# Routed experts: only the filled slots of a tile are gathered and stored, by indirect transfers with a bound

## The chip, the cores and the metric

The kernel is one program on one core of a Trainium2 chip. The core has five engines with a queue each: PE (matrix multiply into PSUM), DVE (VectorE), ACT (ScalarE), POOL (GpSimd) and SP (which issues DMAs here). DMAs issued from any of them run on the core's 16 DMA engines. The metric is the device time of one execution in microseconds, as a median of several runs.

## The reference

A long network for 512 tokens of width 1024: a first block (four mixers and a feed-forward part), then two transformer layers over 512 tokens plus, in layer 0, 256 context tokens. Each of the two layers ends in a mixture of experts, and that is all the change touches. Each token goes to two of 16 experts (1024 to 256 to 1024), and all tokens to one shared expert:

```python
idx = grp[:, None] * EXPERTS_PER_GROUP + local          # two experts for each token
wts = wts / jnp.sum(wts, axis=-1, keepdims=True)
combine = jnp.einsum('tk,tke->te', wts, jax.nn.one_hot(idx, N_EXPERTS, dtype=jnp.float32))
y = jnp.einsum('tef,efd->td', jax.nn.silu(g) * u * combine[..., None], prm['w_down'])
y = y + (jax.nn.silu(t @ prm['sh_gate']) * (t @ prm['sh_up'])) @ prm['sh_down']
```

## The kernel before

`moe` runs once for each layer (768 tokens in layer 0, 512 in layer 1). `route` (from L1899) sorts the pairs of token and expert into tiles of 128 slots: tile s < 16 belongs to expert s, its filled slots first; pairs beyond the 128th of an expert go to overflow tiles, of which layer 0 always runs one (tile 16) and a loop `For_i` (L2184) any further ones. It makes two tables: `idx` (L1997), for each slot of each tile the token whose row it takes, with token 0 in empty slots, and `sli` (L1975), for each token and each of its two experts the slot that holds its result.

`expert` (L2018 to L2069) is a generator in three parts for one tile. First POOL gathers 128 rows of `h2` (4 KB each, in DRAM) into `xe` by an indirect DMA (L2025), PE transposes them in eight pieces (L2039) and ACT and DVE split each into a high and a low part. Then the gate and up weights are loaded by `wpart` (SP, L2082, two halves of 512 KB into one buffer of 1 MB), split likewise (ACT L208, DVE L209), and multiplied in three products for each pair of parts (`mm3`, L186 to L188). Then the down weights, and the result `ye` of 128x1024, which ACT copies out of PSUM (L2067) and SP stores to `yslot`, a DRAM tensor with one row for each slot (L2068). The loop in `moe` (L2168 to L2180) interleaves the parts of neighbouring tiles, and in six tiles of layer 0 and four of layer 1 a piece of the shared expert's product (`shared_down`). The weights have several buffers, so SP issues loads as early as a buffer is free; SP's queue runs in the order in which it was written, and so does POOL's.

Behind the loop, `gather(t)` (L2196) fetches for each token tile the two rows of each token from `yslot` by two indirect DMAs on POOL (L2199), and ACT and DVE weigh and add them (L2207 to L2210). In layer 0 `l1_open` goes on to the next norm (scale rows `nsc`, loaded by POOL); in layer 1 the sum is stored as the output and the kernel ends. Empty overflow slots are read by nobody's result, but `zeros` fills their rows of `yslot` at the start (L1850). Instructions are put in order by a scheduler that honours data dependences and priorities.

## Time and profile before

| | us |
|---|---|
| median of 3 runs | 2537.07 |
| lowest and highest of them | 2532.33, 2540.72 |
| the profiled execution | 2529.52 |
| its span, first to last instruction | 2527.8 |

Engine times are sums of busy time over the span; a PE instruction's busy time runs to the modelled end of its pipeline, so neighbours overlap. Idle time is shown with what ended it. The times of the sections below are from the profiled execution, in microseconds from the start of the span.

### The profile page before, as it was taken

The page shows a single profiled execution, that of the slowest core. Times are in us where ns is not written, and L with a number is a line of the kernel's source. Part 1 is how long each engine was busy: PE and PEld are TensorE (multiplying, and loading weights), DVE is VectorE, ACT ScalarE, POOL GpSimd, SP SyncE. Part 2 cuts the span into 40 slices and gives each one's busy share as a digit, 9 for nine tenths or more (in the row PEclk, how much of TensorE's full clock was granted, in tenths as well). Part 3 has the DMA queues.
Part 4 walks back from the last instruction along what each step waited for, and adds up shares of the span by engine and source line. Part 5 has one row for each costly group of instructions (what it writes and reads, how often), then busy time and mean ns, then how long its engine had stood idle before and what let it go on. Part 6 is the DMA issues. An engine that isn't in the chain of part 4 may idle for free. (4 is left out here: it accounts for less than half of the span.)

```text
span 2527.8 us, 37507 instructions
## 1 busy us (share of the span) xinstructions
PE 2277.4 (90%) x14345; PEld 1808.3 (72%) x14345; DVE 1545.7 (61%) x2915; ACT 1109.3 (44%) x1836; POOL 321.7 (13%) x409
## 2 busy tenths in 40 slices
PE   8959999999988999988999998898994989998994
PEld 6836577888876677766788886697773767687773
DVE  4455654323324455645676648967876987666885
ACT  4435533212223233433445433336774456624773
POOL 0001201000000000011111114200113113301112
PEclk9979989999999999955999999989997999998997
DMA  5345535233325656453545426639996220056995
GB/s 166 100 166 173 190 136 196 88 109 100 101 61 189 224 191 218 125 125 73 113 112 124 102 59 183 236 130 341 342 340 225 97 67 1 1 171 206 375 365 191
DMA packets 367793, 411.55 MB, mean 163 GB/s; under 512 B 117476, under 2 KB 299172, under 8 KB 361468
## 3 DMA queue, kind: packets, MB, share of 16 engines
q1 hardware_dynamic: 356972, 370.83, 46.4%
q0 software_dynamic: 10640, 38.31, 4.1%
q8 instruction: 114, 1.87, 0.3%
q14 instruction: 67, 0.55, 0.1%
HBM read 340.46 MB, written 70.65 MB: 163 GB/s over the span
## 5 line engine op out<-in xcount | busy, mean ns | idle before, releaser
L304 DVE TENSOR_REDUCE mx<-s 128x1 f32<-128x768 f32 (+4 forms) x160 | 121.4, 760 | 85.9 <-PE s L188 65.3
L209 DVE TENSOR_TENSOR eg_l<-eg_w,eg_h 128x2048 fp32r<-128x2048 f32 x66 | 151.0, 2289 | 19.5 <-ACT eg_h L208 19.3
L208 ACT ACTIVATE eg_h<-eg_w 128x2048 fp32r<-128x2048 f32 x66 | 126.5, 1918 | 28.7 <-DMA eg_w<-in_moe_w_up_dram 12.2
L186 PE MATMUL p<-lhh,abw_hi 128*128 128x512 f32 (+1 forms) x336 | 115.3, 343 | 0.8 <-ACT l0n1tmp L241 0.8
L188 PE MATMUL p<-lhh,abw_lo 128*128 128x512 f32 (+1 forms) x336 | 114.5, 341 | 1.6 <-DVE abw_lo L209 1.6
L187 PE MATMUL p<-lhl,abw_hi 128*128 128x512 f32 (+1 forms) x336 | 114.7, 341 | 0.0
L187 PE MATMUL g<-eg_l,xh 128*128 128x512 f32 x264 | 107.1, 406 | 5.5 <-DVE eg_l L209 5.0
L186 PE MATMUL g<-eg_h,xh 128*128 128x512 f32 x264 | 107.6, 408 | 3.8 <-ACT eg_h L208 3.8
L188 PE MATMUL g<-eg_h,xl 128*128 128x512 f32 x264 | 104.4, 395 | 0.0
L209 DVE TENSOR_TENSOR ed_l<-ed_w,ed_h 128x2048 fp32r<-128x2048 f32 x33 | 75.6, 2292 | 44.1 <-ACT ed_h L208 44.1
L882 PE MATMUL adaps<-adaw,silu_c 128*32 128x512 f32 x384 | 75.3, 640 | 29.6 <-DMA adaw<-in_ada_w_dram 29.6
L994 POOL COPY ms<-mc 128x2 f32<-128x2 f32 x30 | 9.1, 304 | 635.0 <-ACT mc L989 620.1
L2025 POOL DMA_INDIRECT xe<-h2d,idx x33 | 45.9, 1392 | 310.0 <-PE x L2039 243.4
L186 PEld LDWEIGHTS p<-lhh,abw_hi 128*128 128x128 f32 (+1 forms) x336 | 61.8, 184 | 23.9 <-issue 8.0
L310 POOL TENSOR_SCALAR ap<-ap,rc 128x768 f32<-128x768 f32 x64 | 58.4, 913 | 153.7 <-DVE rc L307 92.0
L310 POOL TENSOR_SCALAR mlp<-mlp,rc 128x768 f32<-128x768 f32 (+1 forms) x48 | 41.5, 864 | 250.8 <-DVE rc L307 200.4
L186 PE MATMUL p<-h2h,wg_hi 128*128 128x512 f32 x176 | 69.5, 395 | 0.6 <-ACT h2h L234 0.6
L188 PEld LDWEIGHTS p<-lhh,abw_lo 128*128 128x128 f32 (+1 forms) x336 | 62.3, 185 | 10.1 <-DVE abw_lo L209 2.0
L187 PE MATMUL p<-h2l,wg_hi 128*128 128x512 f32 x176 | 69.1, 393 | 0.0
L188 PE MATMUL p<-h2h,wg_lo 128*128 128x512 f32 x176 | 69.0, 392 | 0.0
L186 PE MATMUL p<-wd_hi,ah 128*128 128x512 f32 x176 | 68.5, 389 | 0.2 <-DVE x L836 0.2
L186 PE MATMUL p<-h2h,wu_hi 128*128 128x512 f32 x176 | 68.7, 390 | 0.0
(750 smaller groups left out, 6770.4 us busy)
## 6 DMA issues: line engine op xcount, KB each, us to landing
adaw<-in_ada_w_dram SPq DMA_DIRECT2D x48, 1024.0 KB
eg_w<-in_moe_w_gate_dram SPq DMA_DIRECT2D x66, 512.0 KB
eg_w<-in_moe_w_up_dram SPq DMA_DIRECT2D x66, 512.0 KB
ed_w<-in_moe_w_down_dram SPq DMA_DIRECT2D x33, 1024.0 KB
yslot<-ye SPq DMA_DIRECT2D x33, 512.0 KB
wg_w<-in_w_gate_up_dram SPq DMA_DIRECT2D x11, 1024.0 KB
wu_w<-in_w_gate_up_dram SPq DMA_DIRECT2D x11, 1024.0 KB
wd_w<-in_w_down_dram SPq DMA_DIRECT2D x10, 1024.0 KB
```

The lines of the kernel that those rows point to most:

```text
L186: mm(out, lh, rh, start=start, stop=False)
L187: mm(out, lh, rl, start=False, stop=False)
L188: mm(out, ll, rh, start=False, stop=stop)
L208: self.nc.scalar.activation(hi, raw, AF.Copy)
L209: self.nc.vector.tensor_sub(lo, raw, hi.bitcast(F32))
L304: nc.vector.tensor_reduce(mx, s, axis=AX.X, op=OP.max, negate=True)
L310: nc.gpsimd.tensor_scalar(pout, pout, rc, 1.0, op0=OP.mult, op1=OP.mult)
L882: nc.tensor.matmul(self.ada_ps[32 * j:32 * j + 32], self.silu_c[:, k], w[:, j * 512:(j + 1) * 512], start=k == 0, stop=k == 7, tile_positi ...
L994: nc.gpsimd.tensor_copy(s[:, a:b:b - a - 1], c[:, a + 1:b - 1:b - a - 3])
L2025: nc.gpsimd.indirect_dma_start(out=x, out_offset=None, in_=h2, in_offset=bass.IndirectOffsetOnAxis(ap=idx, axis=0))
```

## The change

The tables become one: `idx` holds for each slot the output row 2 x token + choice (`idx[:, 1]`) and half of it, the token (`idx[:, 0]`); an empty slot gets 8191, beyond the bound. The gather skips rows beyond the bound. The two buffers `xe` are made once for each layer and cleared, since skipped rows keep what they held. The result is written from POOL by an indirect DMA with a bound, straight to row 2 x token + choice of `yrow` (1536 rows). The combination then needs no indices: one DMA of 1 MB from SP for each token tile brings both rows of each token. The zero fill of `yslot` goes.

```diff
@@ -1845,9 +1845,7 @@
-        self.yslot = self.dram.tile([27 * P, D], F32, name="yslot")
-        for i in range(16, 27):
-            nc.gpsimd.dma_start(self.yslot[i * P:(i + 1) * P], z)
+        self.yrow = self.dram.tile([2 * 768, D], F32, name="yrow")
@@ -1855,8 +1853,8 @@
                                 compare_op=OP.is_gt, fill=0.0)
-        self.tokid = self.ct([P, 6], "tokid")
-        nc.gpsimd.iota(self.tokid, pattern=[[P, 6]], base=0, channel_multiplier=1,
+        self.rowid = self.ct([P, 2, 6], "rowid")
+        nc.gpsimd.iota(self.rowid, pattern=[[1, 2], [2 * P, 6]], base=1, channel_multiplier=2,
                        allow_small_or_imprecise_dtypes=True)
@@ -1971,8 +1969,9 @@
         nc.vector.tensor_reduce(sl, so, axis=AX.X, op=OP.add)
-        sli = pool.tile([P, 2, nt], I32, name="sli")
+        sli = wp.tile([P, 2, nt], I32, name="sli")
         nc.vector.tensor_copy(sli, sl)
@@ -1985,7 +1984,7 @@
                                 count[:, None, :27].to_broadcast([P, n, 27]), op=OP.is_equal)
-        nc.vector.tensor_mul(til, til, self.tokid[:, None, :nt, None].to_broadcast([P, 2, nt, 27]))
+        nc.vector.tensor_mul(til, til, self.rowid[:, :, :nt, None].to_broadcast([P, 2, nt, 27]))
         ip = self.pt("r")
@@ -1993,8 +1992,13 @@
             nc.tensor.matmul(ip[:, :27], row[:, i % 4], tf[:, i], start=i == 0, stop=i == n - 1)
-        idx = pool.tile([P, 27], I32, name=f"idx{l}")
-        nc.vector.tensor_copy(idx, ip[:, :27])
+        rows = wp.tile([P, 2, 27], F32, name="rrows")
+        nc.vector.tensor_copy(rows[:, 0], ip[:, :27])
+        nc.vector.tensor_scalar(rows[:, 1], rows[:, 0], 0.0, 8192.0, op0=OP.is_equal, op1=OP.mult)
+        nc.vector.scalar_tensor_tensor(rows[:, 0], rows[:, 0], -1.0, rows[:, 1], op0=OP.add, op1=OP.add)
+        idx = pool.tile([P, 2, 27], I32, name=f"idx{l}")
+        nc.vector.tensor_copy(idx[:, 1], rows[:, 0])
+        nc.vector.tensor_scalar(idx[:, 0], idx[:, 1], 1, None, op0=OP.arith_shift_right)
@@ -2013,17 +2017,17 @@
         nc.vector.tensor_copy(eidi, eid)
-        return wts, sli, eidi, idx
-
-    def expert(self, l, h2, idx, e, ydst, wp, wq):
+        return wts, eidi, idx
+    def expert(self, l, h2, tok, row, nt, e, wp, wq):
...
         raws, parts, xs = wq
-        p, n0 = xs[self.slots % len(xs)]
+        x = xs[self.slots % len(xs)]
         self.slots += 1
-        x = p.tile([P, D], F32, tag="xe", bufs=n0, name="xe")
         nc.gpsimd.indirect_dma_start(out=x, out_offset=None, in_=h2,
-                                     in_offset=bass.IndirectOffsetOnAxis(ap=idx, axis=0))
+                                     in_offset=bass.IndirectOffsetOnAxis(ap=tok, axis=0),
+                                     bounds_check=nt * P - 1, oob_is_err=False)
@@ -2065,7 +2069,8 @@
             nc.scalar.activation(y[:, ns], py, AF.Copy)
-        nc.sync.dma_start(ydst, y)
+        nc.gpsimd.indirect_dma_start(out=self.yrow, out_offset=bass.IndirectOffsetOnAxis(ap=row, axis=0), in_=y,
+                                     in_offset=None, bounds_check=2 * nt * P - 1, oob_is_err=False)
         yield
@@ -2140,7 +2145,11 @@
         with self.pool(f"route{l}", 1, other) as wp, self.pool(f"shx{l}", 1, other) as wp2:
-            wts, sli, eidi, idx = self.route(l, ps, nt, pool, wp, one)
+            xs = [wx.tile([P, D], F32, name=f"xe{i}") for i in range(2)]
+            for x in xs:
+                nc.gpsimd.memset(x, 0.0)
+            wts, eidi, idx = self.route(l, ps, nt, pool, wp, one)
             sd = self.shared(l, sw or self.shared_w(l), hi, lo, nt, wp2, sp)
@@ -2152,7 +2161,7 @@
             wq = ([(wr, "x", x)] * x + [(wh, "y", y)] * y + [(self.wpool, "", 3)] * 3,
-                  [(self.wpool, "", 2)] * 2 + [(wh, "x", 1)], [(wx, 2)])
+                  [(self.wpool, "", 2)] * 2 + [(wh, "x", 1)], xs)
             self.parts = 0
@@ -2163,7 +2172,7 @@
                     e = bass.ds(v, 1)
-                return self.expert(l, h2, idx[:, s:s + 1], e, self.yslot[s * P:(s + 1) * P], wp, wq)
+                return self.expert(l, h2, idx[:, 0, s:s + 1], idx[:, 1, s:s + 1], nt, e, wp, wq)
@@ -2183,10 +2192,10 @@
                 e = nc.values_load(eidi[0:1, bass.ds(i + one, 1)], min_val=0, max_val=15)
-                ii = wp.tile([P, 1], I32, tag="ovi", name="ovi")
-                nc.vector.tensor_copy(ii, idx[:, bass.ds(i + (16 + one), 1)])
-                for _ in self.expert(l, h2, ii, bass.ds(e, 1), self.yslot[bass.ds(i * P + (16 + one) * P, P), :], wp,
-                                     wq):
+                ii = [wp.tile([P, 1], I32, tag=f"ovi{j}", name="ovi") for j in range(2)]
+                for j in range(2):
+                    nc.vector.tensor_copy(ii[j], idx[:, j, bass.ds(i + (16 + one), 1)])
+                for _ in self.expert(l, h2, ii[0], ii[1], nt, bass.ds(e, 1), wp, wq):
                     pass
@@ -2194,11 +2203,9 @@
             def gather(t):
-                ys[t] = [wp.tile([P, D], F32, tag=f"cy{i}", bufs=4, name="cy") for i in range(2)]
-                for i in range(2):
-                    nc.gpsimd.indirect_dma_start(
-                        out=ys[t][i], out_offset=None, in_=self.yslot,
-                        in_offset=bass.IndirectOffsetOnAxis(ap=sli[:, i, t:t + 1], axis=0))
+                y = wp.tile([P, 2, D], F32, tag="cy", bufs=4, name="cy")
+                nc.sync.dma_start(y, self.yrow[2 * t * P:2 * (t + 1) * P].rearrange("(p i) d -> p i d", i=2))
+                ys[t] = [y[:, 0], y[:, 1]]
```

**POOL, the first tiles of layer 0** (`xe_14674` and `xe_14675` are the two gathered tiles; the names after "waits" are semaphores: DMASW of POOL's own DMAs, DMAHW of SP's, the others of engines). Before, 17 gathers stood in a row:

```order
L1907 IOTA count 128x128
L2025 DMA xe<-h2d,idx_14787 128x1024 [waits DMAHW5_49,DMAHW2_49,DMAHW7_49,DMAHW1_49,DVE_49]
L2025 DMA xe<-h2d,idx_14787 128x1024
L2025 DMA xe<-h2d,idx_14787 128x1024 [waits DMASW3_49,PE_49]
L2025 DMA xe<-h2d,idx_14787 128x1024 [waits DMASW4_49,PE_49]
```

Now, from the memsets on:

```order
L2151 MEMSET xe_14674 128x1024 [waits DVE_49,PE_49]
L2151 MEMSET xe_14675 128x1024
...
L2028 DMA xe_14674<-h2d,idx_14784 128x1024 [waits DMASW2_49,PE_49]
L2028 DMA xe_14675<-h2d,idx_14784 128x1024 [waits DMASW3_49,PE_49]
L2072 DMA yrow<-ye,idx_14784 1536x1024 [waits Activation_49]
L2028 DMA xe_14674<-h2d,idx_14784 128x1024 [waits DMASW4_49,PE_49]
L2072 DMA yrow<-ye,idx_14784 1536x1024 [waits DMASW6_49,Activation_49]
L2028 DMA xe_14675<-h2d,idx_14784 128x1024 [waits DMASW5_49,PE_49]
L2072 DMA yrow<-ye,idx_14784 1536x1024 [waits DMASW0_49,Activation_49]
```

Six gathers stand ahead of the first scatter, then one scatter and one gather take turns; each scatter but the first waits for ACT and for a DMA of POOL, the scatter before.

**SP, the loads of layer 0's experts.** Before, a store of `ye` stood among the weight loads of each tile:

```order
L2082 DMA ed_w<-in_moe_w_down_dram 128x2x1024
L2068 DMA yslot<-ye 128x1024
L2082 DMA eg_w<-in_moe_w_gate_dram 128x4x256
L2082 DMA eg_w<-in_moe_w_up_dram 128x4x256
L2082 DMA eg_w<-in_moe_w_gate_dram 128x4x256
L2082 DMA eg_w<-in_moe_w_up_dram 128x4x256
L2082 DMA ed_w<-in_moe_w_down_dram 128x2x1024
L2068 DMA yslot<-ye 128x1024
```

Now the same rows without those of L2068 follow each other, and behind the loop six loads `cy<-yrow` (four in layer 1) stand in SP's queue.

**DVE, the end of layer 1's routing** (`eg_l` is the low part of the first expert's weights, `r` the PSUM tile with the sorted indices). Before:

```order
L1997 CAST idx_20558<-r_20545 128x27
L2003 RECIPROCAL rws<-rws 128x4
L209 TENSOR_TENSOR eg_l<-eg_w,eg_h 128x2048
L2005 TENSOR_TENSOR wts<-rww,rws 128x8
L209 TENSOR_TENSOR sal_20590<-sga,sah_20588 128x256
```

Now:

```order
L1996 COPY rrows<-r_20591 128x27
L2007 RECIPROCAL rws<-rws 128x4
L209 TENSOR_TENSOR eg_l<-eg_w,eg_h 128x2048
L1997 TENSOR_SCALAR rrows<-rrows 128x27
L2009 TENSOR_TENSOR wts<-rww,rws 128x8
L209 TENSOR_TENSOR sal_20641<-sga,sah_20639 128x256
L1998 SCALAR_TENSOR_TENSOR rrows<-rrows 128x27
L2000 CAST idx_20608<-rrows 128x27
L2001 TENSOR_SCALAR idx_20608<-idx_20608 128x27
```

The token table, which the first gather reads, is now ready four instructions of its own and three of others later.

## Rows read from the trace of the kernel before

**Rows 1.** The page: busy us and instructions by engine; the queue of POOL's DMAs.
```profile
PE 2277.4 (90%) x14345; PEld 1808.3 (72%) x14345; DVE 1545.7 (61%) x2915; ACT 1109.3 (44%) x1836; POOL 321.7 (13%) x409
...
q0 software_dynamic: 10640, 38.31, 4.1%
```

**Rows 2.** Windows of the expert loops: busy us by engine, granted clock, DMA share, GB/s.
```profile
1740.00:1860.00 120.00, 118.12 (x559) 95.04 (x559) 104.72 (x96) 89.48 (x98) 16.75 (x11) 1.00 1.00 349
1860.00:1905.00 45.00, 39.63 (x168) 30.18 (x166) 31.09 (x25) 29.86 (x32) 0.00 (x0) 0.96 0.89 308
2340.00:2460.00 120.00, 117.91 (x561) 95.23 (x560) 104.91 (x94) 90.38 (x99) 15.80 (x10) 1.00 1.05 372
2460.00:2485.00 25.00, 23.25 (x102) 17.68 (x101) 18.25 (x15) 16.64 (x19) 0.00 (x0) 1.00 0.72 246
```

**Rows 3.** POOL's timeline, both expert stages: start, us, what, idle time before and releaser.
```profile
1846.80 2.22 POOL L2025 DMA_INDIRECT xe<-h2d,idx  x1 [7.55 <-PE x L2039]
1856.55 2.62 POOL L2025 DMA_INDIRECT xe<-h2d,idx  x1 [7.54 <-PE x L2039]
1917.80 0.95 POOL L2199 DMA_INDIRECT cy<-yslot,sli  x1 [58.64 <-DMA yslot<-ye]
...
1920.01 0.60 POOL L145 DMA_DIRECT2D nsc<-modrow  x1
...
2308.44 2.42 POOL L2025 DMA_INDIRECT xe<-h2d,idx  x1 [32.60 <-DVE rws L2003]
...
2498.04 0.95 POOL L2199 DMA_INDIRECT cy<-yslot,sli  x1 [52.88 <-DMA yslot<-ye]
```

**Rows 4.** SP's timeline late in layer 0's loop: DMA issues.
```profile
1866.73 2.33 SPq L2082 DMA_DIRECT2D eg_w<-in_moe_w_gate_dram  x1
1877.18 0.36 SPq L2068 DMA_DIRECT2D yslot<-ye  x1
1877.58 0.43 SPq L2082 DMA_DIRECT2D eg_w<-in_moe_w_up_dram  x1
```

**Rows 5.** Windows of 5 us there (columns as rows 2).
```profile
1875.00:1880.00 5.00, 4.92 (x26) 3.89 (x24) 3.30 (x2) 4.67 (x6) 0.00 (x0) 1.00 0.44 127
```

**Rows 6.** ACT's timeline late in the loops and at the end.
```profile
1882.68 1.91 ACT L208 ACTIVATE eg_h<-eg_w 128x2048 fp32r<-128x2048 f32 x1 [1.75 <-DMA eg_w<-in_moe_w_up_dram]
...
2475.23 1.92 ACT L208 ACTIVATE eg_h<-eg_w 128x2048 fp32r<-128x2048 f32 x1 [2.37 <-DMA eg_w<-in_moe_w_up_dram]
...
2502.37 1.15 ACT L2207 ACTIVATE cy<-cy,wts 128x1024 f32<-128x1024 f32 x1 [7.74 <-DMA cy<-yslot,sli]
```

**Rows 7.** Window of the zero fill (columns as rows 2).
```profile
400.00:410.00 10.00, 10.00 (x46) 8.29 (x45) 1.38 (x2) 2.38 (x2) 6.46 (x13) 1.00 1.00 360
```

**Rows 8.** The gathered tile xe: ns min/median/max of its gathers, and their landing.
```profile
L2025 POOL DMA_INDIRECT xe<-h2d,idx x33: 947/975/2847, 1698.4 to 2443.0; - x33
...
DMA to landing us min/median/max: 4.4/7.3/9.6
```

**Rows 9.** PE's timeline at the start of both expert loops.
```profile
1706.86 1.47 PE L2039 MATMUL x<-ident,xe 128*128 128x128 f32 x12
...
2316.38 3.67 PE L2039 MATMUL x<-ident,xe 128*128 128x128 f32 x16 [8.93 <-DMA xe<-h2d,idx]
```

**Rows 10.** DVE's timeline at the three places of the change.
```profile
1925.99 1.28 DVE L2208 SCALAR_TENSOR_TENSOR cy<-cy,wts 128x1024 f32<-128x1024 f32 x1 [14.59 <-DMA nsc<-modrow]
...
2307.49 0.19 DVE L1997 CAST idx<-r 128x27 int32<-128x27 f32 x1 [1.58 <-PE r L1995]
...
2307.68 2.26 DVE L209 TENSOR_TENSOR eg_l<-eg_w,eg_h 128x2048 fp32r<-128x2048 f32 x1
...
2309.93 0.42 DVE L209 TENSOR_TENSOR sal<-sga,sah 128x256 fp32r<-128x256 f32 x1
...
2504.60 1.28 DVE L2208 SCALAR_TENSOR_TENSOR cy<-cy,wts 128x1024 f32<-128x1024 f32 x1 [14.95 <-DMA cy<-yslot,sli]
```

**Rows 11.** The chain that ended last: start, us, what.
```profile
2495.17 2.61 DMA yslot<-ye
```

## The prediction

> **What bounds the kernel now.** I read the page first: PE is busy for 90% of the span [rows 1]. Nothing there says what limits the two stretches that the change touches, so next I read the windows of the expert loops. Layer 0 runs its experts from about 1707 to 1914 us, layer 1 from 2316 to 2495 us. In the steady part of both, PE is busy 118.1 of 120 us at a granted clock of 1.00 and the DMA engines are busy too, share 1.00 to 1.05 at 349 to 372 GB/s [rows 2]. Two limits lie on top of each other, so the question is which ends last. POOL's timeline answers for the late tiles, which carry no piece of the shared expert: gathers follow each other in 9.75 us (1846.80 to 1856.55 us), each released by PE's transposes [rows 3]. PE's own work is that long, so there PE sets the pace. Only after 1860 us does PE lose time in layer 0: 39.63 busy of 45 us [rows 2].
>
> SP's timeline shows why. The gate half of a weight load goes out at 1866.73 us; the up half of the same buffer goes out at 1877.58, because the store of y stands between them in SP's queue and waits until 1877.18 for y [rows 4]. The DMA engines meanwhile fall to a share of 0.44 [rows 5]. ACT then waits 1.75 us for that up half, and 2.37 us for one like it in layer 1 [rows 6].
>
> What the expert loops can give back is thus PE's idle time in them: 1.88 + 5.37 us in layer 0 and 2.09 + 1.75 us in layer 1 (length of each window less PE busy, [rows 2]), 11.1 us in all. Behind each loop lies an exposed stretch: store of the last y, reading of the rows, combination on DVE.
>
> **The change part by part.**
>
> *Zero fill.* Eleven POOL DMAs of 512 KB at 401 us go. PE is busy 10 of 10 us there with the DMA share at 1.00 [rows 7]; PE's work hides the copies. I count 0; were the cover gone they would cost 5.77 MB at that row's 360 GB/s, 16 us.
>
> *Bytes in the loops.* 33 tiles of 128 slots ran [rows 8], 4224 rows; the tokens fill 2 x 768 + 2 x 512 = 2560. The 1664 empty rows, 4 KB each, are neither read nor written any more: 640 in layer 0 (5.2 MB both ways), 1024 in layer 1 (8.4 MB). At 349 and 372 GB/s that is 15 and 22.6 us of DMA time, but PE's pace caps what it can buy at the 11.1 us above.
>
> *Stores leave SP's queue.* The second order piece shows that nothing waiting for y stands between weight loads any more. This goes for the same 11.1 us, above all the 5.37 + 1.75 us late in the loops. Bounds for both edits together: 0 and -11.1 us. The rows nearest are the two waits of ACT, which are plainly of this kind, while several of PE's idle pieces may be ACT's and DVE's own order; I take 60%, **-6.5 us**.
>
> *Stores enter POOL's queue.* The first order piece: scatter s stands ahead of gather s+6. That gather needs transposes that come later on PE than y of s, so nothing new waits for the scatter to be issued; a gather has two tiles of time to land. Each scatter also waits for the one before it (the DMASW wait), since all write one tensor. A POOL DMA takes a median of 0.975 us on POOL and 7.3 us to land [rows 8]; with 0.3 us between, 8.6 us is below 9.75. I count 0, with the slow rival below as the upper end. POOL was idle 7.5 us before each gather [rows 3], which covers the issue. Beside DVE work the same gather took 2.42 us of POOL instead of 0.95 [rows 3].
> The Trainium skill, page "SBUF — State Buffer", section "SBUF: two separate sides", says that a DMA issued from GpSimd has to have its descriptors written by GpSimd, which DVE locks out for the length of some instructions, and advises SP's queue. That speaks against this change: if every scatter took the 2.42 us of that row, a link would be 2.42 + 7.3 + 0.3 = 10.0 us, 0.27 us over PE's pace, on 23 tiles +6 us. Most rows here stay near 0.95 us, so the sum goes without it.
>
> *Indices.* Four more DVE instructions per layer. Layer 0's gather is not waited for (its transposes follow the shared expert's matmuls with no idle time before them, [rows 9]). In layer 1 PE waits 8.93 us for the first gather [rows 9]. There the third order piece puts idx behind the 2.26 us split of eg_l, sal (0.42 us) and four small instructions at 0.19 us, the nearest row being the cast's own [rows 10]: some 3.4 us later. In return the gather no longer collides with that split, 2.42 back to 0.95 us, and the second gather ends soon after either way. Bounds 0 and +3.4; I take **+1.0 us**.
>
> *Memsets.* Two of 128x1024 per layer on POOL, ahead of tri and count, far ahead of the first gather (POOL sat idle 32.60 us before layer 1's, [rows 3]; layer 0 is alike): 0.
>
> *End of layer 1.* The last store took 2.61 us [rows 11]. A scatter takes at least 4.4 us, the shortest landing of a gather [rows 8]: +1.8. Before, POOL issued at 2498.04 and DVE began combining at 2504.60 [rows 3, 10]: 6.6 us. Now one 1 MB load: 2.61 us for the first half as in the store's row, 1.4 for the second at 372 GB/s, then ACT's 1.15 us [rows 6]: 5.1 us, -1.5. After that DVE and POOL run back to back as before. Sum **+0.3 us**, bounds -2 and +5 (a landing of 9.6).
>
> *End of layer 0.* Same +1.8 for the scatter. DVE began at 1925.99 us [rows 10]; now it starts with the scale row that POOL loads behind the loop, which goes out 2 us earlier (1917.80 against 1920.01, [rows 3]) but shares the engines with four 1 MB loads from SP. I take **+1.0 us**, bounds -2 and +5.
>
> Sum: -6.5 + 1.0 + 0.3 + 1.0 = -4.2 us. The profiled execution took 2529.5 us, so 2525.3 there. It lies 7.5 us below the median of the runs shown (2537.07); against the median the forecast is **2533 us**. A measurement of this kernel can tell about 0.3%, 7.6 us, from no change.
>
> **The rivals.**
> *Full relief (25%).* DMA rather than PE's order causes all the idle time in the loops. For it: share 1.00 to 1.05. Against: PE at 98% in the steady part. Then -11.1 + 1.0 + 0 = about -10 us, 2527; with both ends 2 us better as well, 2523.
>
> *No relief (15%).* The filled slots of a tile are its first rows. If the 16 DMA engines share a tile by partition, the engines of the low rows keep nearly their whole load, and each weight load still ends with them; or a skipped row costs its time anyway. What stays is the freed SP queue, about half, -3, and +2.3 for the rest: 2536. The traffic total alone can't tell this; ACT's waits for eg_w can.
> The Trainium skill, page "DMA: Bandwidth & Descriptors", section "The descriptor swizzle", has GpSimd's direct 128-partition transfers dealt to the engines by partition, rows 0 to 63 on eight of them; no run shown here shows engines apart, and by it this rival is the likelier half of the loop's saving.
>
> *The chain of scatters, slower (13%).* A scatter waits on POOL for the landing of the one before. From a landing of 8.5 us on (9.75 - 0.95 - 0.3), POOL and not PE paces a tile, and gathers queue behind. At a gather's slowest, 9.6 us [rows 8], a link is 10.85 us, 1.1 us over, on the 11 + 12 tiles without a shared piece: +25 us, 2563. For it: writes to DRAM at a busy time, now from POOL. Against: the median of 7.3 us, and fewer rows to move.
>
> **How the numbers follow.** The forecast has 47%. Its own range is 2527 to 2540 (loops -11.1 to 0, ends +-2 each, index +-1, not all at once). Faster by over 0.3% means below 2529.5: most of full relief and a fifth of the forecast, 0.34. Slower means above 2544.7: the chain and some of the upper bounds of the two ends, 0.15. The rest, 0.51, is the same. The range for 8 in 10 runs from 2522 (full relief with good ends) to 2546, which leaves out the chain and little else.
>
> **What the changed profile would show.** Right: between the halves of a weight load nothing waits for y any more; q0's bytes fall from 38.31 MB [rows 1] by the zeros (5.77), 20 gathers of result rows (two for each of ten token tiles, 10.49) and the 1664 empty rows read (6.82), and gain 10.49 of scatters, to about 25.7 MB; PE's idle time late in the loops is down to a third; layer 1's first gather is issued 2 to 3 us later relative to the routing matmuls; DVE starts each combination within 2 us of the old delay after the last y. Wrong: POOL waits in front of scatters for the previous one; ACT still waits for eg_w halves by as much; the ends grow by more than 5 us.

## The result, and the profile after

The changed kernel takes 2554.92 us (median of 7 runs, 2548.67 to 2561.14) against 2536.78 us of the kernel before on the same chip (7 runs): ratio 1.0071 [1.0050, 1.0091]. It is slower by some 18 us; 2533 had been forecast, with 2522 to 2546 as the range. The profiled executions stand at 2548.67 and 2529.52 us, 19.1 us apart.

The page's first lines say little about it. PE is busy 6 us longer with the same number of instructions, and the bytes of POOL's queue fell as foreseen, to 25.74 MB:

```profile
PE 2283.6 (90%) x14345; PEld 1805.8 (71%) x14345; DVE 1544.5 (61%) x2923; ACT 1107.3 (43%) x1836; POOL 371.3 (15%) x415
...
q0 software_dynamic: 10928, 25.74, 2.7%
```

The difference shows when the span is cut at the same instructions in both traces, read from PE's timelines. **A** runs from the first matmul with `wg_hi` to the last with `wd_hi` (a dense layer with constant weights, which the change does not touch); **B** is layer 0's expert loop, from its first transposes of `xe` to the last matmul with `ed_h`; **C** goes from there to the last matmul with `gw_hi` and `l1hh`, and holds the combination of layer 0; **D** is layer 1's loop; **E** goes from its last `ed_h` matmul to the end of the span. In us:

| kernel | A | B | C | D | E |
|---|---|---|---|---|---|
| before | 364.5 | 206.0 | 131.8 | 177.0 | 34.4 |
| after | 374.5 | 209.2 | 138.6 | 177.8 | 33.5 |
| after less before | +10.0 | +3.2 | +6.8 | +0.8 | -0.9 |

The five add up to +19.9 us of the +19.1. More than half of it lies in A, where no line was edited. The rest of the program differs from run to run by several us in either direction with the granted clock, in kernels that agree there; so below a kernel is judged by its ratio and its cause by the stage.

**The expert loops.** These windows answer to [rows 2] (same columns: busy us of PE, PEld, DVE, ACT, POOL, granted clock, DMA share, GB/s), moved by the offset of the loops:

```profile
1751.00:1871.00 120.00, 115.61 (x535) 92.75 (x534) 99.90 (x92) 84.36 (x94) 39.98 (x21) 0.97 0.97 332
1871.00:1916.00 45.00, 39.62 (x178) 30.71 (x177) 36.86 (x30) 33.41 (x36) 11.92 (x6) 1.00 0.74 258
2360.00:2480.00 120.00, 118.16 (x561) 94.92 (x560) 104.65 (x94) 90.17 (x100) 41.45 (x22) 1.00 0.99 330
2480.00:2505.00 25.00, 22.20 (x99) 17.09 (x98) 17.72 (x15) 15.66 (x19) 6.40 (x3) 1.00 0.50 167
```

The DMA share fell in all four (1.00 to 0.97, 0.89 to 0.74, 1.05 to 0.99, 0.72 to 0.50). PE's idle time did not: 4.39 + 5.38 + 1.84 + 2.80 = 14.4 us, where it was 11.1. Bytes were saved, and PE's idle time in these windows did not fall with them.

### The profile page after: what moved, and what is told of

Its sections match the earlier page's. It is cut to its first block, busy times and chain, and to the rows that moved or that the text cites. A ratio compares the mean times of both kernels' runs of the same rounds, so it can differ in the third digit from the quotient of the medians.

```text
span 2546.9 us, 37584 instructions
## 1 busy us (share of the span) xinstructions
PE 2283.6 (90%) x14345; PEld 1805.8 (71%) x14345; DVE 1544.5 (61%) x2923; ACT 1107.3 (43%) x1836; POOL 371.3 (15%) x415
## 3 DMA queue, kind: packets, MB, share of 16 engines
q0 software_dynamic: 10928, 25.74, 2.7%
## 5 line engine op out<-in xcount | busy, mean ns | idle before, releaser
L209 DVE TENSOR_TENSOR eg_l<-eg_w,eg_h 128x2048 fp32r<-128x2048 f32 x66 | 150.6, 2287 | 15.5 <-ACT eg_h L208 15.3
L209 DVE TENSOR_TENSOR ed_l<-ed_w,ed_h 128x2048 fp32r<-128x2048 f32 x33 | 75.6, 2292 | 56.0 <-ACT ed_h L208 56.0
L2072 POOL DMA_INDIRECT yrow<-ye,idx x33 | 75.7, 2295 | 197.0 <-ACT ye L2071 170.8
L2071 ACT ACTIVATE ye<-y 128x512 f32<-128x512 f32 x66 | 38.9, 589 | 73.3 <-PE y L188 64.6
L817 DVE TENSOR_TENSOR sg<-sg,p 128x512 f32<-128x512 f32 x22 | 15.1, 688 | 91.2 <-PE p L188 91.2
```

The lines of the kernel that those rows point to most:

```text
L209: self.nc.vector.tensor_sub(lo, raw, hi.bitcast(F32))
L2071: nc.scalar.activation(y[:, ns], py, AF.Copy)
L2072: nc.gpsimd.indirect_dma_start(out=self.yrow, out_offset=bass.IndirectOffsetOnAxis(ap=row, axis=0), in_=y, in_offset=None, bounds_check=2 ...
```

## The experiments

The letters in the expectations name the theories of their batch, each stated where it stands. The parts of the difference were taken one by one: the layout, the end of layer 0, the skipped rows, the store's queue. Ratios are to the kernel before on the same chip.

### A: 32 bytes in front of everything

Lines of PE over the dense layer (420 to 740 us; count, then busy us and mean ns of one, then idle before). Before:

```profile
L186 PE MATMUL p<-h2h,wu_hi 128*128 128x512 f32 x159 | 61.9, 389 | 0.0
```

After:

```profile
L186 PE MATMUL p<-h2h,wu_hi 128*128 128x512 f32 x158 | 62.4, 395 | 0.0
```

The window of 580 to 680 us in the middle, before and then after (columns as above):

```profile
580.00:680.00 100.00, 100.00 (x443) 82.81 (x442) 32.65 (x28) 25.50 (x26) 0.00 (x0) 1.00 0.30 97
```

```profile
580.00:680.00 100.00, 100.00 (x430) 80.35 (x429) 32.58 (x27) 27.29 (x27) 0.00 (x0) 1.00 0.32 106
```

PE never idles, the granted clock is 1.00 (2.4 GHz) in both, and yet 430 matmuls are done in place of 443. By PE's timeline a group of three takes 0.70 us, not 0.68; over 528 groups that is 10.6 us, stage A's +10.0. What the change did to this stage is only to move it: the constant `rowid` (128 x 2 x 6 x 4 B) takes 64 bytes of a partition where `tokid` took 32. In the built program every tile of the dense layer that is allocated behind it from that side lies 32 bytes higher (`h2h` 25568 to 25600, `ah` 66528 to 66560), while the weights, which are allocated from the other side, stay (`wg_hi` and `wd_hi` at 204768, `wu_hi` at 196576).

Three runs tested it. The kernel before with `tokid` padded by 32 bytes and nothing else:

```diff
-        self.tokid = self.ct([P, 6], "tokid")
+        self.tokid = self.ct([P, 16], "tokid")[:, :6]
```

> The kernel before, with nothing changed but its constant tokid padded from 32 to 64 bytes per partition. Theory A (layout): the same run of matmuls slows from 0.68 to 0.70 us per three, the time rises by 9 to 12 us, to some 2547. Rival: no difference to the kernel before, within 3 us.

The changed kernel with `rowid` padded, so that the shift is 64 bytes:

```diff
-        self.rowid = self.ct([P, 2, 6], "rowid")
+        self.rowid = self.ct([P, 24], "rowid")[:, :12].rearrange("p (i t) -> p i t", i=2)
```

> The changed kernel, with its constant rowid padded from 64 to 96 bytes per partition, so that every tile allocated behind it lies 64 bytes (not 32) above its place in the kernel before. Theory A (layout): the long matmul run from 395 to 760 us of the changed kernel takes 0.70 us per three matmuls instead of 0.68, because one operand now starts 32 bytes off the other in units of 64; 528 triples there give 10.6 us. Expected: that pace back to 0.68, and the time 9 to 12 us below the changed kernel, some 2545 us, still 6 to 10 us above the kernel before. Rival (the pace hangs on something else that the change took away, such as the zero fill, or is a state of that one execution): pace and time as in the changed kernel, 2555.

And the changed kernel with a `rowid` of 32 bytes (the choice, 0 or 1, is added where the table is used), so that every tile has its old place:

```diff
-        self.rowid = self.ct([P, 2, 6], "rowid")
+        self.rowid = self.ct([P, 6], "rowid")
...
-        nc.vector.tensor_mul(til, til, self.rowid[:, :, :nt, None].to_broadcast([P, 2, nt, 27]))
+        for i in range(2):
+            nc.vector.scalar_tensor_tensor(til[:, i], self.rowid[:, :nt, None].to_broadcast([P, nt, 27]), float(i),
+                                           til[:, i], op0=OP.add, op1=OP.mult)
```

> The changed kernel with rowid in 32 bytes per partition (24 used; the choice is added in two instructions), so that the tiles of the long matmul run lie exactly where they lay in the kernel before: distance of the two operands a multiple of 1024 bytes, instead of 32 more (the changed kernel) or 64 more (e1_parity, whose pace there changed between 0.687 and 0.700 us per three matmuls). Theory A2 (the distance of the operands sets the pace, and only the old distance gives 0.68): pace 0.680 through the whole run, the stretch from the first wg to the last wd 364 to 365 us as in the kernel before (374.5 in the changed kernel), time 9 to 11 us below the changed kernel: 2544 to 2546. Rival A3 (the pace is a state into which an execution falls, whatever the addresses): a mixture of 0.687 and 0.700 as in e1_parity, 2550.

| kernel | median us | ratio | A | C |
|---|---|---|---|---|
| before, shifted 32 B | 2541.68 | 1.0028 [1.0008, 1.0048] | 375.3 | 131.9 |
| after, shifted 64 B | 2550.79 | 1.0049 [1.0025, 1.0073] | 369.8 | 138.9 |
| after, old places | 2545.88 | 1.0054 [1.0036, 1.0072] | 363.9 | 137.9 |

The same line of PE for the shifted kernel before, and for the changed kernel in the old places:

```profile
L186 PE MATMUL p<-h2h,wu_hi 128*128 128x512 f32 x160 | 63.2, 395 | 0.0
```

```profile
L186 PE MATMUL p<-h2h,wu_hi 128*128 128x512 f32 x153 | 59.5, 389 | 0.0
```

Padding alone makes stage A of the kernel before 375.3 us; the old places give the changed kernel 363.9. So the place of the tiles is the cause of A, both ways round: in all fourteen profiled executions with the old places, those below included, A is 363.6 to 365.2 us. The whole times say it less sharply. Padding alone costs 0.0028, 7 us with 2 to 12 as the interval; the old places bring the changed kernel from 1.0071 to 1.0054, 4 us with overlapping intervals, where A alone fell by 10.6. With 64 bytes it came out between: groups of 0.687 us take turns with groups of 0.700 within one run, and the line of `wd_hi` is still slow where that of `wu_hi` is nearly back:

```profile
L186 PE MATMUL p<-h2h,wu_hi 128*128 128x512 f32 x160 | 62.5, 390 | 0.0
L186 PE MATMUL p<-wd_hi,ah 128*128 128x512 f32 x144 | 57.0, 396 | 0.0
```

With this shift the place does not settle the pace by itself. The next section has a kernel in which every tile has the place that it has here, and in the middle of its dense layer the same matmuls run at 0.700, not 0.687. The window of 580 to 680 us here, then there:

```profile
580.00:680.00 100.00, 100.00 (x438) 82.05 (x438) 34.89 (x28) 29.70 (x29) 0.00 (x0) 1.00 0.30 97
```

```profile
580.00:680.00 100.00, 100.00 (x430) 81.02 (x429) 34.90 (x28) 28.40 (x28) 0.00 (x0) 1.00 0.29 95
```

A is 369.8 us here and 373.2 there, so something besides the place is at work, and no run shows what. Padding to a multiple of 64 bytes is thus no cure; the old place is. Why the place matters stays open. In the old layout the distance between the two operands was a multiple of 1024 bytes (204768 - 25568 = 175 x 1024), but another run of matmuls that the shift brought to such a distance (`lhh` with `abw_hi`) did not become faster, 405 ns before and 410 after, so this is no rule.

### C: six loads ahead of the scale row

POOL's timeline of the changed kernel at the end of layer 0 (start, us, what, idle before and its releaser), then SP's, then DVE's:

```profile
1926.86 0.97 POOL L2072 DMA_INDIRECT yrow<-ye,idx  x1 [4.75 <-ACTq L2193]
1931.01 0.57 POOL L2235 DMA_DIRECT2D ng<-in_norm_g_dram  x1
```

```profile
1929.69 26.18 SPq L2207 DMA_DIRECT2D cy<-yrow  x6
```

```profile
1944.49 1.23 DVE L2236 SCALAR_TENSOR_TENSOR nsc<-nsc,ng 128x1024 f32<-128x1024 f32 x1 [22.89 <-DMA ng<-in_norm_g_dram]
1945.63 1.28 DVE L2215 SCALAR_TENSOR_TENSOR cy<-cy,wts 128x1024 f32<-128x1024 f32 x1
```

SP puts the first four loads of 1 MB into the DMA engines at once, at 1929.69 us. POOL's scale row `ng` goes out 1.3 us behind them and lands 13.4 us after its issue, where it had taken 8.2. DVE, whose first instruction needs it, starts at 1944.49 where 1925.99 [rows 10] plus the 12.5 us by which B ended later would be 1938.5. Before, POOL issued gathers and the rows one after another in a single queue [rows 3], so the small rows were not last. DVE's order had changed as well: before, it began with the sum, and the product with the scale row stood fourth (1929.71 us); now that product stands first, and the sum, whose part from ACT was done at 1936 us, waits behind it. One line puts layer 0's loads back into POOL's queue, once on the kernel shifted by 64 bytes and once on that in the old places:

```diff
-                nc.sync.dma_start(y, self.yrow[2 * t * P:2 * (t + 1) * P].rearrange("(p i) d -> p i d", i=2))
+                (nc.sync if l else nc.gpsimd).dma_start(y, self.yrow[2 * t * P:2 * (t + 1) * P].rearrange("(p i) d -> p i d", i=2))
```

> As e1_parity, and in layer 0 the six loads cy<-yrow are issued by POOL, among the loads of the scale rows as the gathers stood before, instead of by SP. Theory B (queueing at the end of layer 0): in the changed kernel four 1 MB loads of SP stand in the DMA engines ahead of ng (issued 1931.0, DVE waits for it until 1944.5); with the order restored DVE starts the combination 5 to 8 us earlier and the time falls by 5 to 8 us against e1_parity, to some 2538. Rival (DVE is the bound of that stretch anyway and has slack later, or the last scatter is what delays it): within 2 us of e1_parity.

> As e5_same_places, and the loads cy<-yrow of layer 0 issued by POOL among the scale rows, as in e3_scale_first. If theory A2 and theory B (queueing, worth 7 us from the last y of layer 0 to the end of the next projection: 138.9 us in e1_parity, 131.8 in e3_scale_first) are both right and add up, what is left of the change is the two loops, which differ by less than 2 us: 2535 to 2539, the same as the kernel before. If something else is still lost: 2543 or more. If the loops do give the 6.5 us of the forecast: 2530 or less.

Shifted: 2544.23 us, 1.0036 [1.0015, 1.0057], C 138.9 to 131.8. In the old places: 2538.15 us, 1.0018 [1.0000, 1.0035], C 137.9 to 131.7, against 131.8 before. In both, C is back at its old length; the ratios fall by 0.0013 and 0.0036, 3 and 9 us. POOL's and DVE's timelines of the second:

```profile
1923.45 0.59 POOL L2209 DMA_DIRECT2D cy<-yrow  x1 [2.59 <-issue]
1924.59 0.54 POOL L2237 DMA_DIRECT2D ng<-in_norm_g_dram  x1
```

```profile
1929.84 1.28 DVE L2217 SCALAR_TENSOR_TENSOR cy<-cy,wts 128x1024 f32<-128x1024 f32 x1 [15.21 <-ACT cy L2216]
```

`ng` now stands behind one load of 1 MB, and DVE begins with the combination and waits for its data. The edit moved both the loads and DVE's order, so what each of them is worth alone is not shown.

### Do skipped rows pay?

Two runs move the empty slots too: they read row 0 and write to rows behind the real ones (`yrow` gets 256 more), with everything else as in the kernel that they stand beside.

```diff
-        self.yrow = self.dram.tile([2 * 768, D], F32, name="yrow")
+        self.yrow = self.dram.tile([2 * 768 + 2 * P, D], F32, name="yrow")
...
-                                     in_offset=None, bounds_check=2 * nt * P - 1, oob_is_err=False)
+                                     in_offset=None, bounds_check=2 * 768 + 2 * P - 1, oob_is_err=False)
```

> As e1_parity, but empty slots are moved too: they read row 0 of the tokens, and write to rows of their own behind the 1536 of yrow, so 13.6 MB more are moved in the two expert loops. Theory C (in the loops PE and the order of ACT's and DVE's work set the pace, and the skipped rows buy nothing): within 3 us of e1_parity. Rival (the skipped rows do buy the 6.5 us of the forecast, and something else takes them back): 6 us or more above e1_parity. Second rival (scatters with more rows land so late that the chain of scatters sets the pace): 15 us or more above, with POOL waiting for yrow.

> As e6_places_and_order, but empty slots are moved too (as in e4_all_rows: they read row 0 and write to rows behind the 1536). Theory D: the two loops are 2.5 to 4 us longer each than in e6_places_and_order, as e4_all_rows (209.0 and 181.0 us) was against e1_parity (205.7 and 178.4): 5 to 8 us in all. Rival C: within 2 us of e6_places_and_order.

On the kernel shifted by 64 bytes: 2555.51 us, 1.0076 [1.0052, 1.0100], against 2550.79 without; B +3.3, D +2.6. On the kernel in the old places with POOL's loads: 2549.46 us, 1.0063 [1.0039, 1.0087], against 2538.15; B +3.7, D +3.5. Then the kernel before with the bounded gathers alone, stores and combination as they were:

```diff
-        x = p.tile([P, D], F32, tag="xe", bufs=n0, name="xe")
+        x = xs[self.slots % len(xs)]
...
-                                     in_offset=bass.IndirectOffsetOnAxis(ap=idx, axis=0))
+                                     in_offset=bass.IndirectOffsetOnAxis(ap=idx, axis=0),
+                                     bounds_check=nt * P - 1, oob_is_err=False)
```

> The kernel before, with one part of the change alone: gathers with a bound into two cleared buffers; results are stored whole by SP and read back by two gathers, as before. Theory D (a skipped row is worth something while the DMA engines are full, about 3 us for the half that is read, and the scatters on POOL cost what the skipping gives): 2 to 5 us below the kernel before, 2530 to 2533. Rival C (PE, ACT and DVE set the pace and skipped rows buy nothing): within 2 us of the kernel before.

> e7_gather_only once more, unchanged, beside these two and for its interval: its median was 2527.75 us, 0.9982 (0.9965 to 1.0) of the kernel before. Theory D (skipped rows of the gather are worth 3 to 6 us): ratio 0.997 to 0.999 again. Rival C: 1.000.

> e7_gather_only once more, beside h1_best_parts: ratio 0.998 to 0.9985 as in its two runs; if the stages add up, 2 to 3 us above h1_best_parts.

The three gave 0.9982 [0.9965, 1.0000], 0.9984 [0.9967, 1.0001] and 0.9990 [0.9965, 1.0014], mean 0.9985, with B at 200.5, 200.2 and 201.6 us where it was 206.0 before. So skipped rows do buy 4 to 6 us of layer 0's loop by the gathers alone. Of layer 1's loop, where more rows are empty, the gathers alone buy nothing that shows: D is 176.2, 178.3 and 176.6 us, 177.0 before. In the changed kernel, with the same gathers and skipped stores besides, the gain in layer 0 is gone. Something that came with the stores gave it back.

### The store: its form, its queue, or what it leaves behind?

On the kernel with bounded gathers, the store moves to POOL as a plain transfer, then as an indirect one with a bound that writes the slot's own row of `yslot`:

```diff
-        nc.sync.dma_start(ydst, y)
+        nc.gpsimd.dma_start(ydst, y)
```

> As e7_gather_only, with one word changed: the store of ye to its slots is issued by POOL instead of SP, as a plain DMA of the whole tile. POOL's queue then has the order of the changed kernel (six gathers, then a store and a gather in turn), SP's queue has no store. Theory E (it is POOL's queue that costs: gathers behind a store that waits for y; and SP's early loads): both loops as long as in e6_places_and_order (208.5 and 179.7 us against 200.5 and 176.2 in e7_gather_only), the time near 2538. Theory F (it is the indirect form that costs: 2.45 us on POOL and 8 us to land, where SP's store took 2.6): both loops within 1.5 us of e7_gather_only, or shorter as SP is freed, the time 2525 to 2529.

```diff
-        nc.gpsimd.dma_start(ydst, y)
+        nc.gpsimd.indirect_dma_start(out=self.yslot, out_offset=bass.IndirectOffsetOnAxis(ap=row, axis=0), in_=y,
+                                     in_offset=None, bounds_check=27 * P - 1, oob_is_err=False)
```

> As f1_store_by_pool, but the store is an indirect transfer with a bound: filled slots go to their own row of yslot, empty ones nowhere (all 27 tiles of yslot are cleared at the start, 16 more than before, under PE's work). Results are read back by two gathers as in the kernel before. Theory E: no longer than f1_store_by_pool by more than 1.5 us, since the queue is the same and less is written. Theory F: both loops as in e6_places_and_order, 8 and 3.5 us longer than in e7_gather_only, the time 2536 to 2540; ACT waits for yslot in front of ye (3.6 and 2.2 us in e6_places_and_order).

The plain store: 2543.93 us, 1.0032 [1.0019, 1.0046], B 208.3, as slow as the changed kernel (209.2). The indirect one: 2541.01 us, 1.0007 [0.9987, 1.0028], B 205.8. The indirect form is not what costs: the plain one loses more, and holds POOL for a quarter of the time of a scatter (0.587 us; the scatters' 2.45 stand further below). Its tile `yslot` (ns min/median/max of a store):

```profile
L2072 POOL DMA_DIRECT2D yslot<-ye x33: 531/587/600, 1747.2 to 2509.3; - x33
```

The largest stall of B behind its first tiles sits at one place in both kernels: ACT waits 3.47 us for a half of the expert weights, and PE behind it. The changed kernel, ACT, then PE, then the window of 5 us there:

```profile
1856.35 1.91 ACT L208 ACTIVATE eg_h<-eg_w 128x2048 fp32r<-128x2048 f32 x1 [3.47 <-DMA eg_w<-in_moe_w_up_dram]
```

```profile
1858.32 0.80 PE L186 MATMUL g<-eg_h,xh 128*128 128x512 f32 x1 [2.89 <-ACT eg_h L208]
```

```profile
1860.00:1865.00 5.00, 5.00 (x16) 3.94 (x15) 4.64 (x6) 1.58 (x1) 0.00 (x0) 0.54 1.04 374
```

The kernel with the plain store, ACT:

```profile
1853.23 1.91 ACT L208 ACTIVATE eg_h<-eg_w 128x2048 fp32r<-128x2048 f32 x1 [3.47 <-DMA eg_w<-in_moe_w_up_dram]
```

After PE's idle time the granted clock falls to 0.54, near the lower level of 1.2 GHz, so the pause costs more than its own 2.9 us. How much shows against the gathers alone, where ACT does not wait there. ACT's split of the down weights of tile 10 (counted from 0) comes 132.7 us after the loop's start in both; that of tile 11, which follows the stall, 147.5 us with the plain store and 142.4 us without:

```profile
1862.16 1.92 ACT L208 ACTIVATE ed_h<-ed_w 128x2048 fp32r<-128x2048 f32 x1 [0.33 <-PE y L188]
```

```profile
1853.84 1.92 ACT L208 ACTIVATE ed_h<-ed_w 128x2048 fp32r<-128x2048 f32 x1 [0.34 <-PE y L188]
```

So 5.1 of the 7.8 us between these two loops arise at the stall; the rest comes near the loop's end and was not taken apart. Which load was late? Counted back along ACT's order it is the first half of tile 12 (`16422` in the program). SP's order in the changed kernel around it, where `16441` is the second half and `16460` the down weights of the same tile:

```
709 L2087 DMA eg_w_16441<-in_moe_w_gate_2_dram 128x4x256
710 L2087 DMA eg_w_16441<-in_moe_w_up_2_dram 128x4x256
711 L2087 DMA ed_w_16460<-in_moe_w_down_2_dram 128x2x1024
712 L2087 DMA eg_w_16422<-in_moe_w_gate_2_dram 128x4x256
713 L2087 DMA eg_w_16422<-in_moe_w_up_2_dram 128x4x256
```

And its timeline, the same five:

```profile
1837.67 0.37 SPq L2087 DMA_DIRECT2D eg_w<-in_moe_w_gate_dram  x1
1838.08 0.72 SPq L2087 DMA_DIRECT2D eg_w<-in_moe_w_up_dram  x1
1841.72 0.37 SPq L2087 DMA_DIRECT2D ed_w<-in_moe_w_down_dram  x1
1845.07 0.37 SPq L2087 DMA_DIRECT2D eg_w<-in_moe_w_gate_dram  x1
1845.49 0.50 SPq L2087 DMA_DIRECT2D eg_w<-in_moe_w_up_dram  x1
```

The half that is needed first goes out last, behind a half that ACT takes up at 1859.65 us and down weights that it takes up only at 1875.78. The store, which had stood between the loads, was part of what fixed their order; without it the scheduler laid tiles 11 to 15 differently. (Of this part of SP's queue it was said ahead of the prediction that the same rows now follow each other. That was read without the buffers' numbers: the loads themselves had changed places.) Tile 9 has its three loads in this order in the kernel before too, and in neither kernel does ACT wait there: the order makes a half late, but by itself no stall.

If the order of the loads is the cause and not POOL's queue, a plain store by POOL must be harmless once the loads come as they are needed. They do with six weight buffers in layer 0 in place of seven:

```diff
-            x, y = ((2, 2), (3, 0))[l]
+            x, y = ((2, 1), (3, 0))[l]
```

Three kernels got it: that with POOL's plain store, that with the bounded gathers alone (its control), and the mended one (old places, POOL's loads).

> f1_store_by_pool with six weight buffers instead of seven in layer 0's loop; the loads of a tile then stand in SP's queue in the order in which they are needed (first half, second half, down weights). Theory G (the order of loads makes the stall at tile 13): layer 0's loop falls from 208.3 to 201 to 204 us, no idle time of PE over 1.5 us between 100 and 170 us after its start; layer 1's loop, in which nothing is changed, stays at 179. Theory E (POOL's queue): layer 0's loop stays at 207 or more.

> e7_gather_only with the same six buffers, as the measure for g1_pool_store_6: what the missing buffer costs by itself. Both theories: layer 0's loop between 200 and 204 us. If it is over 206, fewer buffers cost too much, and g1_pool_store_6 is to be read against this run alone.

> e6_places_and_order (the changed kernel with the old places and the old order at the end of layer 0) with the six buffers. Theory G: layer 0's loop falls from 208.5 to 201 to 205 us and the time from 2538 to 2531 to 2534, no slower than the kernel before. Theory E: 2537 to 2540.

| kernel | seven buffers | B | six buffers | B |
|---|---|---|---|---|
| gathers, plain store by POOL | 1.0032 [1.0019, 1.0046] | 208.3 | 1.0004 [0.9990, 1.0019] | 197.9 |
| gathers alone, store by SP | 0.9985 (mean of three) | 200.8 | 1.0000 [0.9983, 1.0017] | 204.2 |
| mended | 1.0018 [1.0000, 1.0035] | 208.5 | 0.9987 [0.9970, 1.0004] | 203.4 |

ACT's waits for halves of weights in layer 0's loop (us, times, longest) in the kernel with POOL's plain store, with seven buffers, then with six:

```profile
ACT eg_h L208 <- DMA eg_w<-in_moe_w_up_dram: 4.8, 2, 3.5
```

```profile
ACT eg_h L208 <- DMA eg_w<-in_moe_w_up_dram: 0.6, 1, 0.6
```

The stall is gone where the order is mended, with the same store in the same queue; with SP's store, whose order had been good, six buffers change the order again, ACT waits 2.51 and 3.84 us, and B is up by 3.4. So the stall is not POOL's queue, which costs nothing in layer 0's loop, and it goes with the order of the loads; as the number of buffers changed along with the order, no run shows the order alone. In layer 1's loop the store on POOL may cost something: with skipped rows D is 177.6 to 180.3 us with it and 176.2 to 178.3 with SP's store. The other kernels mostly bear it out. Nine have seven buffers and the store on POOL: in eight of them ACT waits 2.5 to 4.4 us for that half; the ninth (shifted by 64 bytes, loads of POOL) ran without the wait though its loads stand in the same order, with the lowest B of the nine, 204.5. Among the late tiles the longest such wait is at most 1.8 us in the kernels before and with the gathers alone, and at most 0.8 in those with six buffers and POOL's store. Of the size of the loss less is sure: B of the nine scatters from 204.5 to 209.2 us (212.2 with all rows moved), and the 197.9 came at a mean clock of 0.99 in the loop, where the mended kernel has 0.96. A third buffer for `ye`, so that ACT doesn't wait for scatters, was tried on top:

> As g3_mended_6, with a third buffer for ye in both layers (there is room for it in layer 0 now). If ACT's waits for a scatter to land (3.6 and 2.2 us in e6_places_and_order) cost time: 2 to 4 us below g3_mended_6. If they lie beside other waits, as f1_store_by_pool (which has none of them and the same loops) suggests: within 2 us of g3_mended_6.

2533.68 us, 0.9989 [0.9974, 1.0005]: no different from 0.9987. Last, the parts that looked best: six buffers, POOL's plain store in layer 0 and SP's in layer 1 (POOL's plain store had lengthened E to 38.6 and 38.2 us; why was not tried).

> Parts put together: as g1_pool_store_6 in layer 0 (gather with a bound, plain store of ye by POOL, six weight buffers: loop 197.9 us), and as e7_gather_only in layer 1 (store by SP: loop 176.2 and 178.3 us, end 34.5, where g1_pool_store_6 had 179.7 and 38.2). If the stages add up: layer 0's loop 197 to 199 us, layer 1's 176 to 178.5, end 34 to 35, and 2 to 3 us below e7_gather_only: ratio to the kernel before 0.9965 to 0.998. If the scheduler's order of layer 0 changes with layer 1's store, or the measurement hides it: as e7_gather_only, 0.998 to 0.9985.

2538.06 us, 1.0002 [0.9977, 1.0026]. The loops came out as expected, B 198.4 (at a clock of 0.96) and D 176.2 us, and E was 35.9; but in the profiled execution the stretches outside the five stages took some 8 us more than in the kernel before, and in the whole time the parts did not add up. No version tried is surely faster than the kernel before: the best, the gathers alone and the mended kernel with six buffers, stand at 0.9985 and 0.9987 with intervals that reach 1.

## Why the prediction was wrong

The forecast was -4.2 us on the profiled execution, and the five stages give +19.9. Of the 24.1 us between them, 10.0 lie in A, 10.5 in the two loops and 5.8 at the end of layer 0; the indices and the end of layer 1 came out 2.2 better than their terms.

**What no step had.** The place of the tiles: +10 us. The working counted instructions, bytes and queues; that a constant grew by 32 bytes was in the diff and was given no term. Shown by padding alone, and by undoing it.

**End of layer 0: +1.0, measured +6.8.** The step said that the scale row "shares the engines with four 1 MB loads from SP" and put +1.0 on it, with +1.8 for the scatter inside. What it shared was not the price: it landed 13.4 us after its issue, 8.2 before, and the instruction that DVE's order had put first stood still for it. The bound of +5 was too low as well. With the loads in POOL's queue, and DVE's order with them, C is back at 131.7.

**Bytes in the loops and SP's freed queue: -6.5, measured +3.2 in layer 0 and +0.8 in layer 1, with the scatter of B told above.** The bytes were right in kind: in layer 0 the gathers alone bring 4 to 6 us, though in layer 1, where the working counted more empty rows, they bring nothing. The other half, that loads only gain when the store leaves their queue, failed; the order of the loads changed with it and put the needed half last. The order piece ahead of the prediction was read without the buffers' numbers, which would have shown it.

**Terms that held or nearly held.** Zero fill, 0: A is 364.5 with it and 363.9 without it in the old places. Bytes of POOL's queue, 25.7 MB. Stores on POOL's queue, 0, by the six-buffer run, in layer 0's loop; in layer 1's it is open. End of layer 1, +0.3: E fell by 0.9, and DVE starts at 2524.59 instead of 2504.60, 20.0 us later where the loop ended 20.1 later. Indices, +1.0, came out at 0. The routing's last matmuls start 19.2 us later than before and the first gather 22.65 us later, 3.4 us of delay as worked out; but this gather holds POOL for 1.15 us instead of 2.42, and PE starts 4.5 us after its issue instead of 7.9, so the first transposes (2316.38 before) come 19.25 us later. POOL and PE at the start of layer 1:

```profile
2331.09 1.15 POOL L2028 DMA_INDIRECT xe<-h2d,idx  x1 [36.16 <-DVE idx L2001]
```

```profile
2335.63 1.94 PE L2043 MATMUL x<-ident,xe 128*128 128x128 f32 x8 [8.84 <-DMA xe<-h2d,idx]
```

**The rivals.** The chain of scatters ended on the right side for the wrong reason. The scatters' tile `yrow` (ns min/median/max on POOL; landing), and POOL's waits for the one before (us, times, longest):

```profile
L2072 POOL DMA_INDIRECT yrow<-ye,idx x33: 971/2446/2464, 1750.2 to 2514.7; - x33
...
DMA to landing us min/median/max: 2.1/8.3/9.5
```

```profile
POOL yrow L2072 <- DMA yrow<-ye,idx: 5.5, 1, 5.5
```

It waited once in 33. A scatter does take up to 2.45 us of POOL beside DVE's work: in 31 of the 33 a product of DVE of 2.29 us (L209) was running, and the scatter ended 0.8 to 0.9 us after it. The other two, the last of each loop, took 0.97 us with DVE idle, and took the same when all rows were moved. The Trainium skill, page "SBUF — State Buffer", section "SBUF: two separate sides", says that DVE and GpSimd share ports which one of them holds for a whole instruction, also where DVE's instruction has two inputs in SBUF and GpSimd's reads SBUF. By that the scatters agree, but the plain store took 0.587 us beside the same product, and no time hung on either. No relief (2536) failed in its sum and in its mechanism, for skipped rows pay in layer 0. Full relief (2527) fell too.

**What stays open.** Why PE's pace hangs on the place of its operands, and on what else it hangs with the shift of 64 bytes; what the order of the loads costs apart from the number of buffers; and why layer 0's loop in the mended kernel with six buffers (203.4 us) is not at the 200.8 of the gathers alone. In that kernel ACT splits weights in another order at the loop's end too, which was not tried apart.

## What to carry to other kernels

Cut both traces at the same instructions before explaining anything: half of this loss lay in a stage that the change never named, and a pad of 32 bytes in the old kernel shows it in one run. When a transfer leaves a queue, read the order of what stays there with its buffers' numbers, and check that what is needed first is still loaded first. A small load that a whole stage waits for belongs ahead of the bulk loads, in the same queue.

## What was not expected of the chip

PE's pace changed with the place of its operands in SBUF at a full granted clock: 389 ns became 395 for the same matmul, 0.68 us became 0.70 for three, and with another shift 0.687 and 0.700 took turns within one run, and two kernels with the same places differed. An indirect scatter that began beside a DVE product of 2.29 us ended 0.8 to 0.9 us after that product, after up to 2.45 us; with DVE idle it took 0.97 us, while a plain store took 0.587 us beside the same product.
